# Moving split weights to other SBUF offsets, and streaming tokens in permuted orders in the FFN

## The chip, the cores and the metric

The kernel runs on one NeuronCore of a Trainium2 chip. The metric is the device time of one execution in microseconds (us). Three runs of the kernel before took 1754.56, 1755.35 and 1756.45 us; the median is 1755.35 us. The engines are PE (TensorE; its weight loads are shown apart as PEld), DVE (VectorE), ACT (ScalarE), POOL (GpSimd) and SP (SyncE, which issues nearly all loads).

## The reference, cut to what matters

One layer over 256 tokens of width 2048: two layer norms, modulation from a conditioning vector, grouped-query attention with a window and a context, a convolution branch, gates, a merge, and a SwiGLU feed-forward part of width 5632. All arrays are float32. Nearly all of the arithmetic is in the matrix products, of which the change touches these:

```python
proj = h @ w_in                                   # q, k, v, GLU (a, gt), gates (ga, gc)
y_attn = attn_flat @ lp['w_attn_proj']            # ap
y_conv = conv @ lp['w_conv_proj']                 # cp
mix = (g_attn * y_attn + g_conv * y_conv) @ lp['w_out']      # wo
g, u = jnp.split(h2 @ w_ffn_in, 2, axis=-1)       # fg, fu
ffn = (jax.nn.silu(g) * u) @ w_ffn_out            # fo
```

## The kernel before, in words

Every float32 product is made from three products in float32r (float32 with a shorter mantissa for PE). Each operand is split into `hi`, a copy rounded to float32r (ACT, line 229 for weights, 124 for tokens), and `lo`, the rest (DVE, line 232 or 125). PE then adds hi·hi, hi·lo and lo·hi in PSUM.

The weights come as a stream of units. A unit is 1 MB: four blocks of 128 rows by 512 columns, or two of 128 by 1024. SP loads a unit in two halves into `raw` tiles; ACT and DVE split each half into one tile `hi` and one tile `lo` of 128 partitions by 1024 words. Each of the two kinds has four such slots (`whi`, `wlo`), so two units are split ahead of the one that PE works on. A Python planner writes the order of all engines out: after each unit it places the splits of the unit two ahead and so much convolution work for DVE (`BUDGET`, some 3 us a unit) and rows of the modulation (`ROWS`). The order on each engine is fixed by this; nothing is chosen at run time.

There are two ways to multiply:

- `mm_ws` (lines 248 to 256): the weight block of 128 by 128 is stationary, and the 256 tokens stream through: 48 matmuls of 256 columns for each unit. It serves gt, a, ga, ap, gc, cp and the FFN's fg and fu. The FFN has 22 chunks of 512 columns in the order fg0, fu0, fg1, fu1 and so on to fu10, each of four units.
- `mm_as` (lines 234 to 246): 128 tokens are stationary, and 512 weight columns stream. It serves q and wo, and with two blocks of 512 the last product fo. `kv_piece` (lines 501 to 503) does the same for K and V, once on the tokens (`hhi`, `hlo`) and once on the context (`hc`).

Each matmul has its own weight load, which runs beside the matmul before it. So at any time PE reads two places of SBUF: the operand that streams, and the stationary operand of the next matmul. The start addresses in the built program, modulo 256 bytes, are as follows. All blocks within a tile lie at multiples of 512 bytes, so one number stands for a tile. "Difference" is the stationary operand's start less the streaming one's, modulo 256.

| products | streams | stationary | difference before | difference after |
|---|---|---|---|---|
| gt, a, ga, ap, gc, cp | tokens at 32 | weights at 224, after 96 | 192 | 64 |
| fg, fu: chunks 0 to 15 | tokens at 32 | weights at 224, after 96 | 192 | 64 |
| fg, fu: chunks 16 to 21 | tokens at 32 | weights at 224, after 80, 88, 92, 100, 104, 112 | 192 | 48, 56, 60, 68, 72, 80 |
| q, wo, kv | weights at 224, after 32 | tokens at 32 | 64 | 0 |
| kvc (context) | weights at 224, after 32 | `hc` at 224, after 32 | 0 | 0 |
| fo | weights at 224 | tokens `hr` at 224 | 0 | 0 |
| last products fol, by pieces | weights at 32 or 224 | tokens at 224 or 32 | 192, 0, 64 | 192, 0, 64 |

In the last two pieces of the last product (lines 1015 to 1027, 256 columns each, named `fol`) the weights of units that were kept earlier (`hl`, at 32) stand before those of the ordinary slots (`hi`, `lo`, at 224).

Of the kernel before, what the change touches and what calls it, by code (L numbers as in the profile page):

```python
# [16 lines left out]
P = 128  # L17
# [35 lines left out]
ROWS = (60, 35, 0, 45, 50, 70, 60, 25)
ROW_GAP = 2
G1_PE_ROWS = 8
Z_GAP = 4
# The end: units of the last product held back, and the pieces of the last columns and stores.
LATE = 5
LAST_COLS = ((0, 512), (512, 256), (768, 256))
OUT_COLS = (((0, 1024), (1024, 1024)), ((0, 512), (512, 512), (1024, 512), (1536, 256), (1792, 256)))  # L60
SCHED = {ET.PE, ET.SP, ET.DVE}

# [26 lines left out]
def layer(ctx, tc, x, c, cx, c_ctx, w_mod, b_mod, w_in, attn_sink, conv_w, conv_b, conv_norm_g, conv_norm_b,  # L89
# [36 lines left out]

# [1 line left out]
    cst = cp.tile([P, 1026], F32, name="cst")  # L128
# [40 lines left out]

# [1 line left out]
    units = []  # L171
# [19 lines left out]
    def unit(kind, src, work, post=None, shape=(P, 4, 512)):  # L191
        u = Unit()
        u.kind, u.src, u.work, u.post, u.shape = kind, src, work, post, list(shape)
        u.after, u.fill, u.extra, u.keep, u.direct = [], None, 0.0, False, False
        units.append(u)
        return u
# [15 lines left out]
    def emit_split(u, i, half, defer_lo=False):  # L212
        nk, nc_ = u.shape[1:]
        h = max(1, nk // 2)
        a = h * half
        if half == 0:
            u.hi, u.lo = [], []
            if u.keep:
                u.both = t16([P, 2, nk, nc_], f"hl{i}", F32R)
        if u.keep:  # L220
            hi, lo = u.both[:, 0, a:a + h], u.both[:, 1, a:a + h]
        else:
            hi = sb.tile([P, h, nc_], F32R, name=f"hi{i}_{a}", tag="whi", bufs=2 * SPLITS)
            lo = sb.tile([P, h, nc_], F32R, name=f"lo{i}_{a}", tag="wlo", bufs=2 * SPLITS)
        u.hi += [hi[:, k] for k in range(h)]
        u.lo += [lo[:, k] for k in range(h)]
        src = u.raw[half]
        with tc.high_priority(offset=URGENT):
            act.activation(hi, src, AF.Copy)  # L229
            if defer_lo:  # L230
                return lambda: dve.tensor_sub(lo, src, hi.bitcast(F32))
            dve.tensor_sub(lo, src, hi.bitcast(F32))  # L232
# [15 lines left out]
    def mm_ws(ps, xh, xl, k0, u, first, last):  # L248
        for ct, ki in [(ct, ki) for a in (0, 2) for ct in range(4) for ki in (a, a + 1)]:
            cs = slice(P * ct, P * ct + P)  # L250
            o = ps[ct // 2][:, 256 * (ct % 2):256 * (ct % 2) + 256]
            k, l = k0 + ki, last and ki == 3
            pe.matmul(o, u.hi[ki][:, cs], xh[:, k, :], start=first and ki == 0 and ct % 2 == 0, stop=False,  # L253
                      skip_group_check=True)
            pe.matmul(o, u.hi[ki][:, cs], xl[:, k, :], start=False, stop=False, skip_group_check=True)  # L255
            pe.matmul(o, u.lo[ki][:, cs], xh[:, k, :], start=False, stop=l, skip_group_check=True)  # L256

    def chunk(lst, mul, w, c0, x2, post, name, rate=0, late=False):
# [3 lines left out]
        for q in range(4):  # L262
# [39 lines left out]

# [1 line left out]
    def load_x(src, name):  # L304
# [97 lines left out]

# [1 line left out]
    def mod_head(k0, kind):  # L404
# [39 lines left out]
    def modulate(k0, srcs=(1, 0)):  # L444
        if hT[0] is None:
            hT.v = [t16([P, KT, SEQ], "hhi", F32R), t16([P, KT, SEQ], "hlo", F32R)]
        ks = slice(k0, k0 + 2)
        for s in srcs:
            src = ("x", "ctx")[s]
            if s == 0:  # L450
                hi, lo = hT[0][:, ks, :], hT[1][:, ks, :]
            else:
                if k0 == 0:
                    env["hc"] = t8([P, 2, 2, 2, SEQ], "hc", F32R)
                hi, lo = (env["hc"][:, k0 // 2 % 2, i] for i in range(2))
            xT = env[src + "T"]
            tmp = sg(f"hm{s}{k0}", (P, 2, SEQ))
            for i in range(2):
                k = k0 + i
                dve.tensor_scalar(tmp[:, i, :], xT[:, k, :], scv[:, k, s:s + 1], shv[:, k, s:s + 1],  # L460
                                  op0=OP.mult, op1=OP.add)
            hi_lo(hi, lo, tmp)

# [1 line left out]
    def rope(dst, ps, t):  # L465
# [52 lines left out]
    def kv_unit(k0):  # L518
        order = ((0, 1), (0, 0), (1, 1), (1, 0))

        def work(u):
            for kind, s in order:
                for i in range(2):
                    pieces.append(lambda kind=kind, s=s, i=i: kv_piece(u, k0, i, kind, s))
        return unit("w", wsrc(w_in, k0, OFF_K, 2, 1024), work, shape=(P, 2, 1024))

# [15 lines left out]

# [1 line left out]
    def q_post(j, ps):  # L544
# [67 lines left out]

# [1 line left out]
    rows_start = {}  # L614

    def mod_row(name, c0):
        n = G1_PE_ROWS if name == "g1" else 0

        def place(k):
            """Column block and quarter of the rows of a unit for the tensor engine."""  # L620
            k -= KT - n
            return k // (n // 4), 4 - n // 4 + k % (n // 4)
# [53 lines left out]

# [1 line left out]
    end_of_slot = []  # L678
# [125 lines left out]

# [1 line left out]
    def ap_post(j, ps):  # L806
# [28 lines left out]

# [1 line left out]
    def renorm_x():  # L837
# [119 lines left out]

# [1 line left out]
    def fg_post(j, ps):  # L959
# [102 lines left out]

# [1 line left out]
    rows_make = {n: mod_row(n, D * i) for n, i in (("g1", 2), ("sh2", 3), ("sc2", 4), ("g2", 5))}  # L1064
# [119 lines left out]

# [1 line left out]
    glu[0].after.append(kv_finish)  # L1186
# [27 lines left out]

# [1 line left out]
    state = {"split": 0}  # L1216
# [96 lines left out]
```

## Time and profile before

| what | value |
|---|---|
| time, median of three runs | 1755.35 us |
| profiled execution, span from the first to the last instruction | 1752.4 us |
| median less span | 2.95 us |
| PE busy / DVE busy / ACT busy | 1710.0 / 1261.8 / 770.4 us |
| mean granted TensorE clock | 0.994 of full |
| matmuls of 256 float32r columns by `mm_ws` | 8784 (lines 253, 255, 256 together) |

The profile states the span of its one execution and no second time for it; what lies around the span is taken as the 2.95 us by which the median is longer. The busy time of a matmul in the profile is a modelled length that overlaps its neighbours (281 ns for one of 256 columns). The rate is read from the distance between two starts, or from the number of matmuls in a window.

### The profile page before, as it was taken

What the parts mean: (1) busy time and instruction counts of PE and PEld (TensorE: products, weight loads), DVE (VectorE), ACT (ScalarE), POOL (GpSimd) and SP (SyncE); (2) the same over time, 40 slices, a digit from 0 to 9 for tenths busy, and PEclk for the clock granted to TensorE, in tenths of its full rate; (3) what the DMA queues carried; (4) which work ended last, traced back from release to release, by engine and by line L of the source; (5) the groups of instructions that cost most, each with busy time, mean ns of one, the idle gap of its engine ahead of it and who ended that gap; (6) DMA issues with size and microseconds to landing.
All of it is one profiled execution on the core that took longest, in us unless ns stands there. A gap on an engine that the chain in (4) does not pass through costs nothing.

```text
span 1752.4 us, 29735 instructions
## 1 busy us (share of the span) xinstructions
PE 1710.0 (98%) x12185; PEld 1545.0 (88%) x12185; DVE 1261.8 (72%) x1698; ACT 770.4 (44%) x949; POOL 7.5 (0%) x8
## 2 busy tenths in 40 slices
PE   5999999999999999999999999999999999999997
PEld 3667999777889999999977899999999999888886
DVE  5446699999998899887898648555555544555766
ACT  3222443366664344466334443434343444444451
POOL 0000000000000000000000000000000000000000
PEclk8999999999999999999999999999999999999999
DMA  9996877643347777876899377777777776555561
GB/s 344 326 330 198 275 253 240 193 120 98 108 121 242 249 267 254 285 265 221 316 353 320 102 228 253 230 239 231 237 231 238 232 227 181 192 192 193 193 226 61
DMA packets 190064, 397.10 MB, mean 227 GB/s; under 512 B 11748, under 2 KB 45540, under 8 KB 188644
## 3 DMA queue, kind: packets, MB, share of 16 engines
q1 hardware_dynamic: 188320, 390.20, 68.0%
q10 hardware_dynamic: 1608, 5.01, 0.7%
q8 instruction: 95, 1.56, 0.4%
q14 instruction: 41, 0.34, 0.1%
HBM read 393.06 MB, written 2.10 MB: 225 GB/s over the span
## 4 chain that ended last, share of the span: by engine, by line
PE 91%; DVE 6%; ACT 1%; DMA 1%; issue 1%; SPq 0%; DVEq 0%; ACTq 0%
PE fu L255 5%; PE fu L253 5%; PE fu L256 5%; PE fg L255 5%; PE fg L256 5%; PE fg L253 5%; PE fo L246 4%; PE fo L243 4%; PE fo L244 4%; PE ap L253 2%; PE ga L253 2%; PE gc L256 2%; PE a L253 2%; PE a L255 2%; PE ap L256 2%; PE gc L255 2%
## 5 line engine op out<-in xcount | busy, mean ns | idle before, releaser
L229 ACT ACTIVATE hi<-raw 128x1024 fp32r<-128x1024 f32 x524 | 554.0, 1059 | 729.4 <-PE fu L255 148.3
L232 DVE TENSOR_TENSOR lo<-raw,hi 128x1024 fp32r<-128x1024 f32 x522 | 635.1, 1222 | 313.3 <-ACT hi L229 309.7
L253 PE MATMUL fu<-h2hi,hi 128*128 128x256 f32 x704 | 197.8, 281 | 0.0
L255 PE MATMUL fu<-h2lo,hi 128*128 128x256 f32 x704 | 196.9, 280 | 0.0
L256 PE MATMUL fu<-h2hi,lo 128*128 128x256 f32 x704 | 196.5, 279 | 0.0
L715 DVE SCALAR_TENSOR_TENSOR y<-ub,cwT,y 128x256 f32<-128x256 f32 x480 | 195.5, 477 | 0.0
L256 PE MATMUL fg<-h2hi,lo 128*128 128x256 f32 x688 | 192.9, 280 | 0.4 <-DVE lo L232 0.4
L253 PE MATMUL fg<-h2hi,hi 128*128 128x256 f32 x688 | 193.3, 281 | 0.0
L255 PE MATMUL fg<-h2lo,hi 128*128 128x256 f32 x688 | 193.2, 281 | 0.0
L253 PEld LDWEIGHTS fu<-h2hi,hi 128*128 128x128 f32 x704 | 132.3, 188 | 0.7 <-issue 0.7
L255 PEld LDWEIGHTS fu<-h2lo,hi 128*128 128x128 f32 x704 | 132.1, 188 | 0.7 <-issue 0.7
L256 PEld LDWEIGHTS fu<-h2hi,lo 128*128 128x128 f32 x704 | 131.8, 187 | 0.0
L253 PEld LDWEIGHTS fg<-h2hi,hi 128*128 128x128 f32 x688 | 130.1, 189 | 0.2 <-issue 0.2
L256 PEld LDWEIGHTS fg<-h2hi,lo 128*128 128x128 f32 x688 | 129.5, 188 | 0.6 <-DVE lo L232 0.6
L255 PEld LDWEIGHTS fg<-h2lo,hi 128*128 128x128 f32 x688 | 129.9, 189 | 0.2 <-issue 0.2
L243 PE MATMUL fo<-hi,hr 128*128 128x512 f32 x320 | 124.5, 389 | 0.0
L244 PE MATMUL fo<-lo,hr 128*128 128x512 f32 x320 | 124.5, 389 | 0.0
L246 PE MATMUL fo<-hi,hr 128*128 128x512 f32 x320 | 98.9, 389 | 0.0
L636 DVE SCALAR_TENSOR_TENSOR g<-raw,csil,g 128x1024 f32<-128x1024 f32 x48 | 61.1, 1283 | 28.0 <-DMA raw<-in_w_mod_dram 27.9
L253 PE MATMUL ga<-hhi,hi 128*128 128x256 f32 x256 | 73.1, 286 | 0.0
L253 PE MATMUL a<-hhi,hi 128*128 128x256 f32 x256 | 72.8, 284 | 0.0
L253 PE MATMUL ap<-ahi,hi 128*128 128x256 f32 x256 | 72.8, 284 | 0.0
(287 smaller groups left out, 3794.4 us busy)
## 6 DMA issues: line engine op xcount, KB each, us to landing
raw<-in_w_in_dram SPq DMA_DIRECT2D x176, 512.0 KB, 4.7
raw<-in_w_ffn_in_dram SPq DMA_DIRECT2D x176, 512.0 KB, 4.6
raw<-in_w_mod_dram SPq DMA_DIRECT2D x128, 512.0 KB, 4.3
raw<-in_w_ffn_out_dram SPq DMA_DIRECT2D x88, 512.0 KB, 3.1
wm<-in_w_mod_dram SPq DMA_DIRECT2D x32, 1024.0 KB, 9.2
raw<-in_w_attn_proj_dram SPq DMA_DIRECT2D x32, 512.0 KB, 6.0
raw<-in_w_conv_proj_dram SPq DMA_DIRECT2D x32, 512.0 KB, 4.7
raw<-in_w_out_dram SPq DMA_DIRECT2D x32, 512.0 KB, 5.8
```

What stands on the lines that cost most here:

```text
L229: act.activation(hi, src, AF.Copy)
L232: dve.tensor_sub(lo, src, hi.bitcast(F32))
L243: pe.matmul(o, a, u.hi[ki][:, js], start=f, stop=False, skip_group_check=True)
L244: pe.matmul(o, a, u.lo[ki][:, js], start=False, stop=False, skip_group_check=True)
L246: pe.matmul(o, b, u.hi[ki][:, js], start=False, stop=l, skip_group_check=True)
L253: pe.matmul(o, u.hi[ki][:, cs], xh[:, k, :], start=first and ki == 0 and ct % 2 == 0, stop=False, skip_group_check=True)
L255: pe.matmul(o, u.hi[ki][:, cs], xl[:, k, :], start=False, stop=False, skip_group_check=True)
L256: pe.matmul(o, u.lo[ki][:, cs], xh[:, k, :], start=False, stop=l, skip_group_check=True)
L636: dve.scalar_tensor_tensor(a, u.raw[n].rearrange("p a b -> p (a b)"), csil[:, k, 0:1], a, OP.mult, OP.add)
L715: dve.scalar_tensor_tensor(y[:, k, :], src, w, y[:, k, :], OP.mult, OP.add)
```

## The change

All of it is in where split weights lie, and in the order in which the FFN's matmuls read tokens.

```diff
+SLACK = 64
+WS_SHIFT, AS_SHIFT, HC_SHIFT = 32, 16, 16
+IN_FORM = {2: (2, 4), 3: (2, 8), 4: (2, 16), 5: (2, 32), 6: (2, 64), 7: (4, 4), 8: (8, 4), 9: (16, 4), 10: (2, 2),
+           11: (4, 8), 12: (4, 16), 13: "pairs", 14: "low"}
+IN_SHIFT = {16: 28, 17: 30, 18: 31, 19: 33, 20: 34, 21: 36}
...
-            hi = sb.tile([P, h, nc_], F32R, name=f"hi{i}_{a}", tag="whi", bufs=2 * SPLITS)
-            lo = sb.tile([P, h, nc_], F32R, name=f"lo{i}_{a}", tag="wlo", bufs=2 * SPLITS)
+            hi, lo = (sb.tile([P, h * nc_ + SLACK], F32R, name=f"{n}{i}_{a}", tag="w" + n, bufs=2 * SPLITS)
+                      [:, u.shift:u.shift + h * nc_].rearrange("p (k c) -> p k c", k=h) for n in ("hi", "lo"))
...
     def mm_ws(ps, xh, xl, k0, u, first, last):
-        for ct, ki in [(ct, ki) for a in (0, 2) for ct in range(4) for ki in (a, a + 1)]:
+        order = [(ct, ki) for a in (0, 2) for ct in range(4) for ki in (a, a + 1)]
+        if u.form:
+            step = 2 if u.form == "pairs" else 1
+            low = (1, 2) if u.form != "low" else (2, 1)
+            for z in range(0, 16, step):
+                for n in (0, *low):
+                    for ct, ki in order[z:z + step]:
+                        o = ps[ct // 2][:, 256 * (ct % 2):256 * (ct % 2) + 256]
+                        x = (xh, xl, xh)[n][:, k0 + ki, :]
+                        if isinstance(u.form, tuple):
+                            o, x = (v.rearrange("p (b a c) -> p a b c", a=u.form[0], c=u.form[1]) for v in (o, x))
+                        pe.matmul(o, (u.hi, u.hi, u.lo)[n][ki][:, P * ct:P * ct + P], x, ...
+            return
+        for ct, ki in order:
...
+            u.shift = WS_SHIFT if mul is mm_ws else AS_SHIFT
...
-                    env["hc"] = t8([P, 2, 2, 2, SEQ], "hc", F32R)
+                    hc = t8([P, 2048 + SLACK // 4], "hc", F32R)
+                    env["hc"] = hc[:, HC_SHIFT:HC_SHIFT + 2048].rearrange("p (a b c s) -> p a b c s", a=2, b=2, c=2)
...
-        return unit("w", wsrc(w_in, k0, OFF_K, 2, 1024), work, shape=(P, 2, 1024))
+        unit("w", wsrc(w_in, k0, OFF_K, 2, 1024), work, shape=(P, 2, 1024)).shift = AS_SHIFT
...
+    for n, u in enumerate(ffn):
+        u.shift, u.form = IN_SHIFT.get(n // 4, WS_SHIFT), IN_FORM.get(n // 4)
...
-    nc = _bacc.Bacc("TRN2", target_bir_lowering=False, num_devices=1)
+    nc = _bacc.Bacc("TRN2", target_bir_lowering=False, num_devices=1, dynamic_dma_scratch_size=8192)
```

Shifts count words of 4 bytes. The slots of split weights grow by 64 words, and the room comes from a DMA scratch area at the start of SBUF, which shrinks from 16,384 to 8,192 bytes. With a form (a, c) a matmul still streams the same 256 tokens, but in another order: words 0 to c-1 of every group of a·c words first, then the next c words of every group, and so on; the output in PSUM is written in the same order, so that every word lands where it did. A form (2, 4) reads runs of 4 words and skips 4. Eleven chunks (2 to 12) have such a form.

All other engines have the same instructions in the same order as before; what moves is on PE in the FFN. The first place is the border of chunk 1 (fu0) and chunk 2 (fg1). `fu01` and `fg10` are PSUM tiles, `h2hi` and `h2lo` the parts of the tokens, `hi240` and so on the parts of the weight unit of that number. Before:

```order
L253 MATMUL fu01_10356<-h2hi_9928,hi240_2_10473 128x256
L255 MATMUL fu01_10356<-h2lo_9929,hi240_2_10473 128x256
L256 MATMUL fu01_10356<-h2hi_9928,lo240_2_10474 128x256
L253 MATMUL fg10_10599<-h2hi_9928,hi241_0_10529 128x256
L255 MATMUL fg10_10599<-h2lo_9929,hi241_0_10529 128x256
L256 MATMUL fg10_10599<-h2hi_9928,lo241_0_10530 128x256
```

And now:

```order
L277 MATMUL fu01_10356<-h2hi_9928,hi240_2_10473 128x256
L279 MATMUL fu01_10356<-h2lo_9929,hi240_2_10473 128x256
L280 MATMUL fu01_10356<-h2hi_9928,lo240_2_10474 128x256
L269 MATMUL fg10_10599<-h2hi_9928,hi241_0_10529 128x2x32x4
L269 MATMUL fg10_10599<-h2lo_9929,hi241_0_10529 128x2x32x4
L269 MATMUL fg10_10599<-h2hi_9928,lo241_0_10530 128x2x32x4
```

The sequence is the same; from chunk 2 on the 256 columns are written as 2 passes over 32 groups of 4 words.

The second place is the border of chunk 13 (fu6, form "pairs") and chunk 14 (fg7, form "low"), on PE as well. Before:

```order
L253 MATMUL fu61_13369<-h2hi_9928,hi299_2_13486 128x256
L255 MATMUL fu61_13369<-h2lo_9929,hi299_2_13486 128x256
L256 MATMUL fu61_13369<-h2hi_9928,lo299_2_13487 128x256
L253 MATMUL fg70_13618<-h2hi_9928,hi301_0_13596 128x256
L255 MATMUL fg70_13618<-h2lo_9929,hi301_0_13596 128x256
L256 MATMUL fg70_13618<-h2hi_9928,lo301_0_13597 128x256
```

And now:

```order
L269 MATMUL fu61_13369<-h2hi_9928,hi299_2_13486 128x256 x2
L269 MATMUL fu61_13369<-h2lo_9929,hi299_2_13486 128x256 x2
L269 MATMUL fu61_13369<-h2hi_9928,lo299_2_13487 128x256 x2
L269 MATMUL fg70_13618<-h2hi_9928,hi301_0_13596 128x256
L269 MATMUL fg70_13618<-h2hi_9928,lo301_0_13597 128x256
L269 MATMUL fg70_13618<-h2lo_9929,hi301_0_13596 128x256
```

In chunk 13 two weight blocks go together through each of the three steps; in chunk 14 the product with the weights' `lo` has moved ahead of that with the tokens' `lo`. The number and size of matmuls stay.

## Rows read from the trace of the kernel before

**Rows 1.** The page: busy time of PE; shares of the chain that ended last.

```profile
PE 1710.0 (98%) x12185; PEld 1545.0 (88%) x12185; DVE 1261.8 (72%) x1698; ACT 770.4 (44%) x949; POOL 7.5 (0%) x8
...
PE 91%; DVE 6%; ACT 1%; DMA 1%; issue 1%; SPq 0%; DVEq 0%; ACTq 0%
```

**Rows 2.** Chain by line in 1070 to 1500, 405 to 446 and 860 to 960 us.

```profile
by line: PE fu L255 17.5%; PE fu L253 17.3%; PE fu L256 17.1%; PE fg L255 15.9%; PE fg L253 15.8%; PE fg L256 15.6%; PE g2b L662 0.8%
...
by line: DVE y L715 38.8%; DVE lo L232 20.3%; DVE sm L575 12.1%; PE pv L602 9.0%; PE s L568 4.2%; DVE s L574 3.6%; issue 3.5%; PE pt L596 2.1%; DVE sm L576 1.7%; DVE rope L476 1.6%; DVE scr L469 1.5%; DVE sm L585 1.2%; DVE sm L584 0.6%; DVE
...
by line: PE wo L244 17.3%; PE wo L246 16.4%; PE wo L243 15.9%; DMA raw<-in_w_conv_proj_dram 10.1%; DVE lo L232 9.9%; issue 8.9%; DVE sc L636 5.8%; PE cp L256 3.6%; PE cp L255 3.2%; PE cp L253 3.2%; DVE m L829 2.4%; DVE gc L828 1.8%; DVE mlo
```

**Rows 3.** Groups by line and shape: out<-in, shape, count | busy, mean ns.

```profile
L253 PE MATMUL fu<-h2hi,hi 128*128 128x256 f32 x704 | 197.8, 281 | 0.0
...
L253 PE MATMUL fg<-h2hi,hi 128*128 128x256 f32 x688 | 193.3, 281 | 0.0
...
L253 PE MATMUL gt<-hhi,hi 128*128 128x256 f32 x256 | 72.8, 284 | 0.0
...
L243 PE MATMUL q<-hi,hhi 128*128 128x512 f32 x128 | 53.6, 419 | 0.0
...
L243 PE MATMUL wo<-hi,mhi 128*128 128x512 f32 x112 | 44.4, 397 | 0.0
...
L501 PE MATMUL kv<-hi,hhi 128*128 128x512 f32 x64 | 26.6, 416 | 0.0
```

**Rows 4.** Windows in the FFN: busy (x count) of PE, PEld, DVE, ACT, POOL; PEclk, DMA, GB/s.

```profile
1070.00:1200.00 130.00, 130.00 (x1106) 130.00 (x1105) 75.82 (x66) 50.97 (x50) 0.00 (x0) 1.00 0.77 245
1200.00:1430.00 230.00, 230.00 (x1950) 229.52 (x1950) 127.79 (x110) 92.98 (x94) 0.00 (x0) 1.00 0.74 236
```

**Rows 5.** PE's timeline: start us, us; 132 matmuls between the first two rows.

```profile
286.02 0.28 PE L256 MATMUL a<-hhi,lo 128*128 128x256 f32 x1
...
300.98 0.28 PE L256 MATMUL a<-hhi,lo 128*128 128x256 f32 x1
```

**Rows 6.** PE's timeline in q (20 between) and in fo (6 between).

```profile
358.26 0.40 PE L246 MATMUL q<-hi,hlo 128*128 128x512 f32 x1
...
362.93 0.40 PE L244 MATMUL q<-lo,hhi 128*128 128x512 f32 x1
...
1560.27 0.39 PE L243 MATMUL fo<-hi,hr 128*128 128x512 f32 x1
...
1561.63 0.39 PE L243 MATMUL fo<-hi,hr 128*128 128x512 f32 x1
```

**Rows 7.** PE's timeline, last pieces: 6 matmuls, 3, then 8 between these rows.

```profile
1738.29 0.28 PE L1022 MATMUL fol<-hl,hr 128*128 128x256 f32 x1
...
1739.01 0.29 PE L1022 MATMUL fol<-hi,hr 128*128 128x256 f32 x1
...
1739.37 0.28 PE L1022 MATMUL fol<-hi,hr 128*128 128x256 f32 x1
...
1740.27 0.28 PE L1026 MATMUL fol<-hi,hr 128*128 128x256 f32 x1
```

**Rows 8.** The chain: eight plain float32 matmuls of 512 columns.

```profile
380.81 3.43 PE pv L602 x8
```

**Rows 9.** DVE's split of weights into ordinary slots and into kept tiles.

```profile
L232 DVE TENSOR_TENSOR lo<-raw,hi 128x1024 fp32r<-128x1024 f32 x522 | 635.1, 1222 | 313.3 <-ACT hi L229 309.7 <-PE ap L255 1.6
...
L232 DVE TENSOR_TENSOR hl<-raw,hl 128x1024 fp32r<-128x1024 f32 x10 | 12.0, 1218 | 1.1 <-ACT hl L229 1.1
```

**Rows 10.** Windows of the stretches in which DVE or the DMA queues are nearly full.

```profile
209.00:285.00 76.00, 76.00 (x646) 75.03 (x644) 70.31 (x107) 30.29 (x31) 0.00 (x0) 1.00 0.75 242
...
313.00:446.00 133.00, 132.53 (x582) 97.55 (x581) 127.40 (x260) 76.03 (x129) 0.00 (x0) 1.00 0.45 130
...
524.00:700.00 176.00, 176.00 (x1467) 168.25 (x1465) 160.65 (x244) 72.41 (x75) 0.00 (x0) 1.00 0.76 253
...
860.00:960.00 100.00, 95.08 (x536) 81.06 (x535) 89.14 (x88) 40.91 (x41) 0.00 (x0) 1.00 0.94 337
```

More of the change, by code (lines that the diff above doesn't have):

```diff
@@ L193, in unit @@
         u.kind, u.src, u.work, u.post, u.shape = kind, src, work, post, list(shape)
-        u.after, u.fill, u.extra, u.keep, u.direct = [], None, 0.0, False, False
+        u.after, u.fill, u.extra, u.keep, u.direct, u.shift, u.form = [], None, 0.0, False, False, 0, None
         units.append(u)
@@ L248, in mm_ws @@
     def mm_ws(ps, xh, xl, k0, u, first, last):
-        for ct, ki in [(ct, ki) for a in (0, 2) for ct in range(4) for ki in (a, a + 1)]:
+        order = [(ct, ki) for a in (0, 2) for ct in range(4) for ki in (a, a + 1)]
[9 more added lines that the diff above has]
+                            o, x = (v.rearrange("p (b a c) -> p a b c", a=u.form[0], c=u.form[1]) for v in (o, x))
+                        pe.matmul(o, (u.hi, u.hi, u.lo)[n][ki][:, P * ct:P * ct + P], x,
+                                  start=first and ki == 0 and ct % 2 == 0 and n == 0,
+                                  stop=last and ki == 3 and n == low[-1], skip_group_check=True)
+            return
+        for ct, ki in order:
             cs = slice(P * ct, P * ct + P)
```

## The prediction

> **What bounds the kernel now.** I read the page first: PE is busy 98% of the span, and 91% of the chain that ended last lies on it [rows 1]. Then the chain by stage: in the FFN it is nothing but PE's own matmuls; at 405 to 446 us (the q products with attention) it runs through DVE; at 860 to 960 us half of it is the wo products, and the rest waits for DMA, DVE and issue [rows 2]. So a shorter step from matmul to matmul shortens nearly the whole span, with two exceptions. Third, the step itself. Busy times of a matmul overlap, so I take distances between starts. In the FFN 1106 + 1950 matmuls of 256 columns fill 360 us: 117.8 ns each [rows 4]. At 286 us the same kind of matmul, with the same shapes and addresses modulo 256, runs at (300.98 - 286.02) / 132 = 113.3 ns, for one stretch [rows 5]; by the starts of all matmuls some 280 of the 8784 run at this step. With 512 columns q takes 4.67 / 20 = 233.5 ns and fo 1.36 / 6 = 226.7 ns [rows 6]. The granted clock is 1.00 in all of these windows, so the clock does not make the difference. PE waits for nobody there: it has two speeds for one shape.
>
> Which speed goes with which difference of start addresses (table in the section on the kernel)? 512 columns: 64 goes with 233.5 ns (q), 0 with 226.7 ns (fo). 256 columns: 192 goes with 117.8 ns, and with 113.3 ns in a few stretches. The last pieces of the last product hold the other two cases of 256 columns [rows 7]: with the kept weights against the second tile of tokens (difference 0) six steps take 0.72 us, 120 ns each; then the ordinary slots begin (difference 64), the first three steps take 0.36 us, and from then on eight take 0.90 us, 113 ns each. The step falls to the low value within three matmuls and stays. So where rows can tell, 64 gives the low step for 256 columns and 0 for 512, and those are the differences the change makes.
>
> **The change part by part.** All sums are against the profiled execution, whose span is 1752.4 us; the median of the runs is 2.95 us more, which I add at the end.
>
> 1. Tokens streaming outside the FFN (gt, a, ga, ap, gc, cp; 192 becomes 64). Six products of 3 x 256 matmuls (gt stands for them) are 4608 [rows 3]; less the 280 that are at 113.3 already, about 4330. Each gains 117.8 - 113.3 = 4.5 ns: -19.3 us. [...] I take the low step that rows show.
>
> 2. FFN chunks in natural order (0, 1, 13, 14, 15; 64). 5 x 192, less 48 of the first unit that never went through `mm_ws`, are 912; -4.1 us. That chunks 13 and 14 take the three products in other order moves when `hi` and `lo` slots come free by one matmul, 0.1 us. ACT and DVE are busy 40% and 56% there (92.98 and 127.79 of 230 us [rows 4]), so it costs nothing; without this cover it would be 0.1 us a unit, 1 us in all.
>
> 3. FFN chunks 16 to 21 (48 to 80), 1152 matmuls. No row shows these differences. Bounds: all at 113.3 (-5.2 us), or none better, up to 120 ns as in the case of difference 0 (+2.5 us). I take half of the gain, -2.6 us.
>
> 4. Weights streaming (q, wo, kv; 64 becomes 0). 3 x 128 + 3 x 112 + 3 x 64 = 912 matmuls of 512 columns [rows 3], each 233.5 - 226.7 = 6.8 ns less: -6.2 us. kvc and fo keep difference 0: nothing.
>
> 5. FFN chunks 2 to 12 in permuted order, 11 x 192 = 2112 matmuls. No matmul of before reads or writes a permuted order, so I bound it. [...] Above: the half rate of plain float32, 429 / 2 = 214.5 ns, +96.7 ns each, +204 us. The nearest rows are the same matmuls in natural order (113.3 to 117.8). I split the forms by run length: six forms read runs of 8 words or more (1152 matmuls), where I take 113.3 ns, -5.2 us; five forms read runs of 2 or 4 words (960 matmuls), where I take today's 117.8, 0 us.
>
> [...]
>
> 6. The splits themselves. ACT and DVE write to shifted tiles. Ordinary slots (raw at 32, parts at 224) take 1222 ns on DVE, kept tiles (all at 32) 1218 ns [rows 9], so the position does not matter to them: 0. The smaller scratch area is not used by any load of this kernel that I can see (SP and ACT issue them all): 0.
>
> 7. What takes some back. Where PE speeds up, DVE must follow in its fixed order. It is busy 127.4 of 133 us in q and 70.3 of 76 us before it [rows 10], and the chain already runs on DVE for 41 us [rows 2]. q's 2.6 us would need DVE at 98%; I count most of that as lost, -2 us of gain. At 860 to 960 us the DMA queues are 94% full [rows 10] and the chain waits for a load, so wo's 2.3 us are mostly lost too. Together +4.5 us. The cover here is small: if it were gone altogether, from 209 to 700 us, see the third rival.
>
> Sum: -19.3 - 4.1 - 2.6 - 6.2 - 5.2 + 4.5 = -32.9 us; 1752.4 - 32.9 + 2.95 = 1722.5 us. Own range: 1711 to 1735, from chunks 16 to 21 and the permuted chunks (either fully at the low step, or some 5 ns above today's).
>
> **The rivals.** First, and on the other side: the permuted orders are slow. Place: chunks 2 to 12, where nothing hides PE (its chain is all matmuls [rows 2]). Price: without the 5.2 us of part 5, the rest gains 27.7 us, so from 27.7 / 2112 = 13 ns above 117.8 on average the kernel is slower than before. If only the five forms with runs of 2 or 4 words fell to the half rate, it would be 960 x 96.7 = +93 us: 1815 us; all eleven, about 1932 us. For it: PE reads at full rate only in whole runs in every row I have, and a step that changes with the offsets alone [rows 6, 7] says that reads of SBUF set it. Against: no row shows it. Chance 0.20.
>
> Second: the change does not do what it says. The 113 ns step appears at difference 192 too [rows 5], so it may be a state that a pause before it sets, not the offset. Then all parts are 0 and the time is 1755. Against: both low steps at the differences 64 and 0 hold to the end of their stretch [rows 6, 7]. Chance 0.07.
>
> Third: DVE becomes the bound wherever it is above 90%, that is from 209 to 700 us. The gain there is 4.5 ns x (646 + 1467 and some 350 between) = 11 us, of which about 1 is counted lost already: 1733 us. For it: 160.65 of 176 us and 70.31 of 76 us [rows 10]. Against: each of these leaves 7 to 9% where PE needs 4%. Chance 0.13.
>
> [...] Chance 0.12.
>
> **How the numbers follow.** The forecast has 0.48. A measurement of this kernel cannot tell less than 0.2%, 3.5 us, from no change. Faster: the forecast, the third and the fourth, 0.73. The second counts 0.05 as the same and 0.02 as slower; the first 0.17 slower, 0.03 the same. So 0.73, 0.08, 0.19. The time is the forecast's, 1722.5 us. The range goes from 1706, a little under the fourth rival, to 1770, which takes in the second and a first rival that costs up to about 47 us on the forecast; below lie some 5%, above some 14%.
>
> **What would show it.** In the new profile gt to cp should step at 113.3 ns in all stages, q and kv at 226.7 ns. Chunks 2 to 12 each have one form and 4 units, so windows of one chunk give its price: 21.8 us at 113.3 ns, 22.6 at 117.8, 41 at half rate. Chunks 16 to 21 should tell which offsets are as good as 64. DVE should stay just under PE from 209 to 524 us, and waits of PE for `lo` should not grow beyond a few us. Wrong it would be if the step at 64 stayed at 118, or any form took over 130 ns.

## The result and the profile after

The changed kernel takes 1769.28 us, median of six runs (1765.74 to 1771.41); the kernel before took 1755.05 us (median of six runs, 1750.72 to 1756.68). The ratio is 1.009, 95% interval 1.0066 to 1.0113: slower, where 1722.5 us was predicted. The profiled execution, the fastest of the six, spans 1764.0 us, 11.6 more than before. The time lies inside the range of 1706 to 1770 us, but in the part that stood for the first rival, not for the forecast.

The page after, its busy times and the shares of the chain [rows 1], and DVE's split of weights [rows 9]:

```profile
PE 1717.8 (97%) x12185; PEld 1553.3 (88%) x12185; DVE 1260.7 (71%) x1698; ACT 770.5 (44%) x949; POOL 7.5 (0%) x8
...
PE 87%; DVE 8%; DMA 2%; ACT 1%; issue 1%; SPq 0%; DVEq 0%; ACTq 0%
...
L241 DVE TENSOR_TENSOR lo<-raw,hi 128x1024 fp32r<-128x1024 f32 x522 | 634.1, 1222 | 331.0 <-ACT hi L238 329.1
```

The instructions are the same in number, and the other engines' busy times within 1.1 us. What changed is the step of PE. Below are windows of the changed kernel: gt1 and a1; ga3 and ap3; chunk 9 (fu4) with form (16, 4); chunk 10 (fg5) with form (2, 2); chunks 14 and 15 in natural order at 64; chunk 16 (fg8) at 48. Columns as in rows 4.

```profile
214.00:254.00 40.00, 40.00 (x356) 40.00 (x355) 39.52 (x60) 16.77 (x17) 0.00 (x0) 1.00 0.78 257
644.96:694.96 50.00, 50.00 (x427) 50.00 (x426) 48.66 (x68) 19.50 (x20) 0.00 (x0) 1.00 0.78 256
1191.00:1215.00 24.00, 24.00 (x180) 24.00 (x179) 11.78 (x10) 8.77 (x9) 0.00 (x0) 1.00 0.69 213
1218.00:1258.00 40.00, 40.00 (x175) 36.24 (x174) 11.86 (x10) 7.40 (x7) 0.00 (x0) 1.00 0.40 122
1329.00:1369.00 40.00, 40.00 (x355) 40.00 (x354) 23.37 (x20) 16.35 (x17) 0.00 (x0) 1.00 0.79 249
1373.00:1393.00 20.00, 20.00 (x172) 20.00 (x171) 11.16 (x10) 7.44 (x7) 0.00 (x0) 1.00 0.77 237
```

A window counts every matmul that reaches into it, two to three more than start in it. With that the first row gives 40 / 353 = 113.3 ns a matmul, the second 117.8, the fourth 40 / 173 = 231 ns: half the rate, with PE busy all the time and the granted clock at 1.00. All steps below are distances between starts, averaged over a chunk without its pauses. The border into chunk 10, the first matmul of chunk 11 and two of q (18 steps apart) on PE's timeline of the changed kernel (start, us):

```profile
351.75 0.40 PE L253 MATMUL q<-lo,hhi 128*128 128x512 f32 x1
...
355.84 0.39 PE L253 MATMUL q<-lo,hhi 128*128 128x512 f32 x1
...
1216.28 0.31 PE L269 MATMUL fu<-h2hi,lo 128*128 128x256 f32 x1
1216.42 0.40 PE L269 MATMUL fg<-h2hi,hi 128*128 128x256 f32 x1
1216.63 0.41 PE L269 MATMUL fg<-h2lo,hi 128*128 128x256 f32 x1
1216.86 0.41 PE L269 MATMUL fg<-h2hi,lo 128*128 128x256 f32 x1
...
1260.55 0.32 PE L269 MATMUL fu<-h2hi,hi 128*128 128x256 f32 x1
```

Chunk 10 takes 1260.55 - 1216.42 = 44.13 us where it took 22.61: +21.52. That alone is nearly twice the loss. q steps at 4.09 / 18 = 227.2 ns (233.5 before [rows 6]).

By the starts of the first matmuls of each stage, after less before, in us, beside the prediction's parts:

| part | predicted | measured |
|---|---|---|
| 1: gt, a, ga, ap, gc, cp | -19.3 | -10.0 (ga and ap together +0.4, the others -10.4) |
| 2: natural chunks 0, 1, 13 to 15 | -4.1 | -3.9 |
| 3: chunks 16 to 21 | -2.6 | +1.0 |
| 4: q and wo; kv | -6.2 | -1.7 and -1.2; kv about 0 |
| 5: permuted chunks 2 to 12 | -5.2 | +27.2 (chunk 10 +21.5, the others +5.7) |
| 7: given back | +4.5 | +1.2 (cp3) |
| loads at the start | 0 | -1.0 |
| sum | -32.9 | +11.6 |

Steps of the permuted chunks, by form (a, c), where c is the length of a run in words and a·c the distance from one run to the next: (2, 4) 117.7 ns, (2, 8) 116.7, (2, 16) 121.3, (2, 32) 120.0, (2, 64) 117.8, (4, 4) 114.5, (8, 4) 126.1, (16, 4) 135.2, (2, 2) 229.9, (4, 8) 119.5, (4, 16) 120.0. The six shifted chunks stand at 117.8 to 120.0 ns.

### The profile page after: what moved, and what is told of

The parts are those of the page before. It is cut to its first block, busy times and chain, and to the rows that moved or that the text cites. A ratio compares the mean times of both kernels' runs of the same rounds, so it can differ in the third digit from the quotient of the medians.

```text
span 1764.0 us, 29735 instructions
## 1 busy us (share of the span) xinstructions
PE 1717.8 (97%) x12185; PEld 1553.3 (88%) x12185; DVE 1260.7 (71%) x1698; ACT 770.5 (44%) x949; POOL 7.5 (0%) x8
## 4 chain that ended last, share of the span: by engine, by line
PE 87%; DVE 8%; DMA 2%; ACT 1%; issue 1%; SPq 0%; DVEq 0%; ACTq 0%
PE fg L269 10%; PE fu L269 8%; PE fo L252 4%; PE fo L253 4%; PE fo L255 4%; PE fu L279 2%; PE fu L280 2%; PE fu L277 2%; DVE y L741 2%; PE ga L277 2%; PE ap L277 2%; PE ga L279 2%; PE ap L280 2%; PE ga L280 2%; PE ap L279 2%; DVE lo L241 2%
## 5 line engine op out<-in xcount | busy, mean ns | idle before, releaser
L241 DVE TENSOR_TENSOR lo<-raw,hi 128x1024 fp32r<-128x1024 f32 x522 | 634.1, 1222 | 331.0 <-ACT hi L238 329.1
L269 PE MATMUL fg<-h2hi,lo 128*128 128x256 f32 x448 | 136.0, 304 | 0.1
L269 PE MATMUL fg<-h2hi,hi 128*128 128x256 f32 x448 | 135.7, 303 | 0.0
L269 PE MATMUL fg<-h2lo,hi 128*128 128x256 f32 x448 | 135.7, 303 | 0.0
L269 PE MATMUL fu<-h2lo,hi 128*128 128x256 f32 x384 | 103.5, 283 | 0.0
L269 PE MATMUL fu<-h2hi,hi 128*128 128x256 f32 x384 | 103.4, 283 | 0.0
L277 PE MATMUL fu<-h2hi,hi 128*128 128x256 f32 x320 | 90.6, 283 | 0.0
L279 PE MATMUL fu<-h2lo,hi 128*128 128x256 f32 x320 | 89.4, 279 | 0.0
L269 PEld LDWEIGHTS fg<-h2hi,lo 128*128 128x128 f32 x448 | 86.1, 192 | 1.7 <-DVE lo L241 0.3
L269 PEld LDWEIGHTS fg<-h2hi,hi 128*128 128x128 f32 x448 | 85.8, 192 | 1.4
L269 PEld LDWEIGHTS fg<-h2lo,hi 128*128 128x128 f32 x448 | 85.8, 191 | 1.4
L280 PE MATMUL cp<-yhi,lo 128*128 128x256 f32 x256 | 71.0, 277 | 1.7 <-DVE lo L241 1.7
```

The lines of the kernel that those rows point to most:

```text
L269: pe.matmul(o, (u.hi, u.hi, u.lo)[n][ki][:, P * ct:P * ct + P], x, start=first and ki == 0 and ct % 2 == 0 and n == 0, stop=last and ki == ...
```

## The experiments

Three questions: what the forms cost by themselves, why (2, 2) is slow, and whether the offset is what makes the low step. In what follows "low" is 113.3 ns and "high" 117.8 ns. Six probes were run once each and are read by chunk from their traces: e3 (1855.57 us), e4 (1736.71), e5 (1736.94), e8 (1749.78), e11 (1858.49) and e12 (1928.49).

**e1: no forms, no shifts.**

```diff
-IN_FORM = {2: (2, 4), ...}
-IN_SHIFT = {16: 28, ...}
+IN_FORM = {}
+IN_SHIFT = {}
```

> The changed kernel with all 22 FFN chunks in natural order at difference 64, as chunks 0, 1 and 15 have it; nothing else differs. Theory F (the forms and the other shifts cost it, the offset gains): every FFN chunk takes 113.3 ns a matmul as chunks 0, 1, 13, 14 and 15 did, so 22 chunks gain 0.85 us each against before and the 24.2 us that the FFN lost are replaced by a gain of 18.4; span 1764.0 - 42.6 = 1721.4 us, ratio to before 0.982. Rival S (the step is a state that is set where PE pauses and then kept; offsets only change the odds): somewhere in the FFN the step goes back to 117.8 ns and stays there; span between 1721 and 1739 us, with chunks of both steps at one difference.

Measured: 1725.64 us (five runs, 1723.09 to 1727.86), ratio to before 0.983 (0.981 to 0.985). All 22 chunks stand at the low step. Windows of ga3 and ap3, and of the FFN, in e1:

```profile
655.00:700.00 45.00, 45.00 (x385) 45.00 (x384) 43.88 (x59) 17.31 (x18) 0.00 (x0) 1.00 0.80 264
1100.00:1350.00 250.00, 250.00 (x2209) 250.00 (x2208) 148.07 (x129) 103.41 (x103) 0.00 (x0) 1.00 0.77 243
```

Theory F holds. The forms and shifts together cost 40 us of span (1764.0 to 1723.8), and the offsets alone gain 28.6 us of span against before, nearly the 32.9 that the prediction had for the whole change. ga and ap stay at the high step here too.

**e2: chunk 10 alone put back, e10: chunk 10 alone changed.** e2 drops one entry of the changed kernel's table; e10 is the kernel before with one chunk permuted.

```diff
 e2
-IN_FORM = {..., 10: (2, 2), ...}
+IN_FORM = {... without 10 ...}
 e10
+            return a.rearrange("p (b a c) -> p a b c", a=2, c=2) if u.form else a
...
+    for u in ffn[40:44]:
+        u.form = True
```

> The changed kernel with one chunk put back: chunk 10 (fg5) in natural order at difference 64 instead of runs of 2 words with hops of 4; the other ten permuted chunks and the six shifted ones stay. Theory F: the form of chunk 10 alone costs 229.9 - 113.3 = 116.5 ns x 192 = 22.4 us, so the span is 1764.0 - 22.4 = 1741.6 us and the ratio to before 0.994: the sign of the result turns. Rival C (the slow stretch is where the step that grew over chunks 7 to 9, 114.5, 126.1, 135.2 ns, would have led in any form): chunk 10 stays above 118 ns and the span above 1750 us.

> The kernel before, and chunk 10 (fg5) alone with runs of 2 words and hops of 4, at before's difference of 192; nothing else differs. Theory R (reading tokens in runs of 2 words halves the rate, whatever the offset): chunk 10 at 229 to 233 ns instead of 117.8, 192 x 112 to 115 = 21.5 to 22.1 us; median 1754.65 + 21.8 = 1776.4 us, ratio 1.0123. Rival (it takes the order and the offset of 64 together): less, down to ratio 1.000.

Measured: e2 1742.81 us, ratio 0.993 (0.990 to 0.996); the sign turns with one chunk of 22. e10 1774.02 us, ratio 1.014 (1.009 to 1.019). Windows of e2 in ga3 and ap3 and in chunk 10; then of e10 in chunks 1, 9 and 10, all at difference 192, the last one permuted:

```profile
652.00:692.00 40.00, 40.00 (x356) 40.00 (x355) 39.85 (x56) 16.34 (x17) 0.00 (x0) 1.00 0.79 269
...
1211.00:1232.00 21.00, 21.00 (x188) 21.00 (x187) 12.62 (x11) 8.82 (x9) 0.00 (x0) 1.00 0.76 238
```

```profile
1021.00:1042.00 21.00, 21.00 (x188) 21.00 (x187) 9.62 (x8) 8.95 (x10) 0.00 (x0) 1.00 0.71 197
1202.00:1223.00 21.00, 21.00 (x181) 21.00 (x180) 11.74 (x10) 8.33 (x9) 0.00 (x0) 1.00 0.76 237
1225.00:1267.00 42.00, 42.00 (x184) 37.95 (x184) 12.29 (x10) 8.04 (x9) 0.00 (x0) 1.00 0.43 129
```

In e2 chunk 10 falls to the low step right behind the slow chunk 9, so rival C is out. Four runs of e2 are two pairs, 1737.60 and 1738.80, 1746.82 and 1747.62; the profiled one is the fastest, with ga and ap at the low step (first row), 6.4 us less there than in the changed kernel. So its median, midway between the pairs, meets the expected 1741.6 us of span by chance; but both pairs lie below all nine runs of the kernel before.

In e10 chunk 10 takes 21.53 us more than in the kernel before, as in the changed kernel: the form does it without the offset and without its neighbours. The first row of e10 holds a surprise: chunk 1 runs at the low step at before's difference of 192.

**e3: the reading and the writing side apart.**

```diff
-                            o, x = (v.rearrange("p (b a c) -> p a b c", a=u.form[0], c=u.form[1]) for v in (o, x))
+                            to, tx = ("p (b a c) -> p a b c" if w in u.form[0] else "p (a b c) -> p a b c" for w in "ox")
+                            o = o.rearrange(to, a=u.form[1], c=u.form[2])
+                            x = x.rearrange(tx, a=u.form[1], c=u.form[2])
```

> A probe: each FFN chunk (192 matmuls) has its own order, all at difference 64, with natural chunks between. In some only the tokens are read in the permuted order (the output columns are written in natural order), in some only the output columns are written in it; such outputs have tokens in other places, so the result isn't the reference's. Runs of 2 words with hops of 4: written side alone in chunk 2, read side alone in 3, both in 5; both sides with hops of 8, 32, 128 and 64 words in chunks 6, 7, 16, 20. Theory R (the read side costs: hops through SBUF halve the rate): chunk 3 at 229 ns, chunk 2 at 113 to 118. Theory W (the written side costs): chunk 2 at 229, chunk 3 at 113 to 118. For hops: if the run of 2 words is what costs, chunks 6, 7, 16 and 20 also stand at 229 ns; if it is the hop of 4 words alone, they stand near 113 to 126. The forms (16, 4) in 9 and 10, (8, 4) in 11 and 12, (2, 16) in 14 and 15, (2, 4) in 18 and 19 split in the same way (reading, writing): the side that costs keeps 135, 126, 121, 118 ns, the other falls to 113.

PE's timeline of e3 at the border from chunk 2, (2, 2) in the written side alone, to chunk 3, in the read side alone; then windows of (16, 4) read (chunk 9) and written (chunk 10):

```profile
1046.26 0.28 PE L272 MATMUL fg<-h2lo,hi 128*128 128x256 f32 x1
...
1047.73 0.28 PE L272 MATMUL fg<-h2hi,lo 128*128 128x256 f32 x1
1047.84 0.39 PE L272 MATMUL fu<-h2hi,hi 128*128 128x256 f32 x1
1048.06 0.41 PE L272 MATMUL fu<-h2lo,hi 128*128 128x256 f32 x1
1048.28 0.41 PE L272 MATMUL fu<-h2hi,lo 128*128 128x256 f32 x1
```

```profile
1271.00:1295.00 24.00, 24.00 (x179) 24.00 (x179) 12.01 (x10) 8.39 (x9) 0.00 (x0) 1.00 0.70 217
1297.00:1317.00 20.00, 20.00 (x179) 20.00 (x178) 11.62 (x10) 7.97 (x9) 0.00 (x0) 1.00 0.77 239
```

Writing in runs of 2 words costs nothing (113.4 ns; the last 13 steps before chunk 3 take 1.47 us), reading in them costs everything (229.8 ns). For (16, 4) reading takes 135.1 ns, writing 113.5. (2, 16) read 121.3, written 113.4; (8, 4) read 126.6 and written at the high step; (2, 4) cannot tell, both sides stand at 117.8. With both sides permuted the hops in between hardly matter: 8 words 233.4 ns, 32 words 233.3, 64 words 226.8; only hops of 128 words give 170.0.

**e12: runs that straddle 16 bytes.** If the length of a run counted, moving it would not matter; if aligned blocks of 16 bytes count, a run of 4 words moved by 2 touches two.

```diff
-                        x = (xh, xl, xh)[n][:, k0 + ki, :]
+                        x = (xh, xl, xh)[n].rearrange("p k s -> p (k s)")
+                        at = SEQ * (k0 + ki) + u.form[2] * (-1 if k0 + ki == KT - 1 else 1)
+                        x = x[:, at:at + SEQ]
```

> A probe at difference 64 (plus what the start shifts): permuted reading from tokens that start 2 words (8 bytes) further in some chunks, so that a run of 4 words no longer lies in one aligned block of 16 bytes but in two; the tokens read are two columns off, so the result isn't the reference's. (2, 2) at start 0 and 2 in chunks 2, 3; (4, 4) at 0, 2, 4, 1 words in 4, 5, 6, 17; natural order 2 words further in 7 and 19, unshifted in 16; (2, 4), (16, 4), (8, 4) 2 words further in 8, 10, 18; (2, 8) at 0 and 2 in 11, 12; (4, 16) at 0 and 2 in 13, 14; (2, 64) and (4, 2) 2 words further in 15, 20. Theory B (PE reads blocks of 16 bytes, and what counts is the blocks that a read touches: twice as many for runs of 2): runs of 4 that straddle touch two blocks each, so chunks 5, 8, 10, 17, 18 go to 226 to 234 ns; runs of 8 that straddle touch 3 instead of 2, about 1.5 x 113 = 170 ns in chunk 12; runs of 16 5 instead of 4, about 142 ns in chunk 14; (2, 2) at 2, natural order and (2, 64) stay. Rival N (the number of runs or the hop counts, not where a run lies): the shifted chunks read as the unshifted, 114 to 135 ns for runs of 4, 117 to 120 for 8 and 16.

Windows of e12: (4, 4) at start 0, at 2 words, at 4 words; (2, 8) at 0 and at 2; (4, 16) at 2:

```profile
1118.50:1138.50 20.00, 20.00 (x177) 20.00 (x176) 11.63 (x10) 7.76 (x8) 0.00 (x0) 1.00 0.71 222
1140.00:1182.00 42.00, 42.00 (x187) 38.54 (x186) 12.97 (x11) 8.37 (x9) 0.00 (x0) 1.00 0.43 132
1184.00:1204.00 20.00, 20.00 (x176) 20.00 (x176) 11.56 (x10) 7.66 (x8) 0.00 (x0) 1.00 0.71 221
1343.00:1364.00 21.00, 21.00 (x182) 21.00 (x181) 12.22 (x11) 7.90 (x8) 0.00 (x0) 1.00 0.68 220
1365.00:1396.00 31.00, 31.00 (x186) 31.00 (x185) 12.55 (x11) 8.51 (x9) 0.00 (x0) 1.00 0.53 170
1421.00:1448.00 27.00, 27.00 (x184) 27.00 (x184) 12.34 (x10) 8.01 (x8) 0.00 (x0) 1.00 0.60 191
```

Theory B holds, in size nearly: (4, 4) goes from 114.6 to 226.5 ns with 2 words and back to 115.1 with 4; with 1 word 232.3; (2, 4) 229.9; (16, 4) from 135.7 to 228.1; (8, 4) to 221.0, below the 226 expected; runs of 8 from 116.8 to 168.4 (170 expected); runs of 16 from 120.0 to 148.0 (142). Natural order was to stay and takes 120.0 and 120.3 ns when moved, against 113.4 unmoved in the same run; the moved start also makes the difference 56, which stood at 117.8 in the changed kernel, and 65 blocks for 64 would make that 119.6. (2, 64) was to stay and went from 117.8 to 128.1; 17 blocks for 16 would be 125.2. (2, 2) stays at 230. So the price of a permuted read is mainly the number of 16-byte blocks that its runs touch. Four words, a whole block, are needed for the full rate: runs of two aligned words stand at 229.9 ns (e11), runs of four at 114.6. The distance between the runs has a part in it that the blocks don't explain: runs of 4 take 114.5 ns at 16 words, 126 at 32 and 135 at 64, and runs of 2 fall from 227 ns at 64 words to 170 at 128 (e3). Why stays open.

**e11: the slow forms at other differences.**

```diff
+IN_FORM = {2: (2, 2), 3: (2, 2), 5: (16, 4), 6: (16, 4), 8: (4, 4), ...}
+IN_SHIFT = {2: 0, 3: 16, 5: 0, 6: 16, ...}
```

> A probe with tokens and output columns in permuted orders at other differences than 64, natural chunks at 64 between: (2, 2) at 192, 0 and 32 in chunks 2, 3, 19; (16, 4) at 192 and 0 in 5, 6; (4, 4) at 64, 0, 32, 128, 192 in 8 to 12; (2, 4) at 0 in 14; (8, 8) and (8, 2) at 64 in 15, 16; (4, 2) and (64, 2) at 0 in 18, 20. Theory R (the run length of what is read decides, the difference is second): runs of 2 words at 229 to 233 ns (170 with hops of 128) at every difference, runs of 4 at the values seen at 64 (117.7, 114.5, 135 ns) give or take 5 ns. Rival (the slow orders come from the difference of 64): at 0 and 192 they fall towards 118 to 120 ns.

Windows of e11 in chunks 2 and 3, (2, 2) at the differences 192 and 0:

```profile
1032.00:1074.00 42.00, 42.00 (x185) 37.94 (x184) 20.82 (x14) 8.10 (x9) 0.00 (x0) 1.00 0.53 177
1076.00:1118.00 42.00, 42.00 (x184) 37.96 (x183) 12.89 (x11) 8.02 (x9) 0.00 (x0) 1.00 0.39 117
```

Theory R holds: (2, 2) takes 229.9, 230.0 and 226.7 ns at 192, 0 and 32; (4, 2) 233.2 at 0; (8, 2) 226.5 at 64; (64, 2) 166.7 at 0. (16, 4) takes 133.4 and 134.7 at 192 and 0; (4, 4) stays between 114.4 and 116.7 at all five differences.

**e4: the difference alone; e5: the whole FFN at 192.** Both change only the table of shifts of e1.

> A probe: all FFN chunks in natural order, chunks at difference 64 alternating with chunks at 192, 0, 128, 32, 96, 160, 224, and at the end a row of 192, 0, 128, 32, 96 without 64 between; nothing else differs from the changed kernel. Theory D (the difference of the start addresses decides): each chunk at 64 takes 113.3 ns, 0 takes 120, 192 takes 117.8, the others 113 to 120 each with one value wherever it stands. Rival S (a state that a pause sets and that PE then keeps): no chunk boundary in the FFN has a pause, so 192 and 0 keep the 113.3 ns with which PE comes into them, and all 22 chunks read the same.

> e1 with one thing put back: all 22 FFN chunks at difference 192, as before had them (the larger slots and everything ahead of the FFN stay as in e1). Theory D (64 and 192 both allow two steps, 113.3 and 117.8 ns, and after a pause of PE 64 comes to rest at the low one, 192 nearly always at the high one): the six entries of the FFN end at 117.8, span 1723.8 + 22 x 0.85 = 1742 us. Rival S (which step is taken is chance at the entry, alike for both differences, and e1 was lucky): the chunks stay at 113.3 or fall into two groups, span 1724 to 1736 us.

Windows of e4 in chunks 3 to 6 (differences 64, 0, 64, 128), then 16 and 17 (192, 0):

```profile
1055.00:1075.00 20.00, 20.00 (x179) 20.00 (x178) 13.35 (x12) 8.39 (x9) 0.00 (x0) 1.00 0.86 292
1077.00:1098.00 21.00, 21.00 (x177) 21.00 (x176) 11.58 (x10) 7.76 (x9) 0.00 (x0) 1.00 0.75 235
1100.00:1121.00 21.00, 21.00 (x181) 21.00 (x179) 11.91 (x10) 8.14 (x9) 0.00 (x0) 1.00 0.75 237
1123.00:1143.00 20.00, 20.00 (x171) 20.00 (x170) 10.96 (x10) 7.42 (x7) 0.00 (x0) 1.00 0.75 234
...
1345.00:1365.00 20.00, 20.00 (x179) 20.00 (x178) 11.60 (x11) 8.10 (x8) 0.00 (x0) 1.00 0.76 242
1367.00:1388.00 21.00, 21.00 (x177) 21.00 (x176) 11.30 (x10) 8.33 (x9) 0.00 (x0) 1.00 0.75 232
```

Each expectation holds by half. 0 takes 120.0 ns both times, 32 118.3, 128 118.7 and 119.0; 160 (120.0) and 224 (116.7) stood once; 96 has two values, 120.0 and 118.7. So at 0, 32 and 128 the difference decides as far as two chunks can tell. But 64 and 192 have two steps. Coming out of the 120 ns of difference 0, chunk 5 at 64 stays high to its end; chunk 16, at 192, enters low and stays low; chunk 2, at 192, enters low and turns high at a pause of 1.6 us. In e4 only the weights move, so it can't tell the difference from the weights' own address; for 64 the last product of the kernel before can, where 113 ns came with other addresses (weights at 224, tokens at 32 [rows 7]). In e5 the six entries of the FFN (one after each pause of PE) all came to rest high: 1736.94 us, one run, 11 more than e1's median though its ga and ap ran low (6.4 us less there than in e1; theory D's 1742 us of span had them high). In e1 the same entries, and a seventh, came to rest low. The same two windows as for e1, in e5:

```profile
655.00:700.00 45.00, 45.00 (x399) 45.00 (x398) 44.00 (x60) 19.20 (x19) 0.00 (x0) 1.00 0.81 273
1100.00:1350.00 250.00, 250.00 (x2125) 250.00 (x2124) 142.95 (x123) 99.07 (x99) 0.00 (x0) 1.00 0.74 233
```

The first row answers a question left by e1: up to the FFN the two kernels are the same program, and here ga3 and ap3 run low, with DVE at 44.00 of 45 us. So neither the offset nor DVE held ga and ap at the high step. In the ten profiles with these stages unchanged (the changed kernel, e1 to e5, e7, e8, e11, e12) ga to ap stood high in six and low in four, and a3 before them the other way round each time. As the program is the same up to there in the changed kernel and in e1 to e5, e11 and e12, it doesn't settle which of the two it is.

**e8: many entries.**

```diff
     def mm_ws(ps, xh, xl, k0, u, first, last):
+        if u.pause:
+            pe.transpose(aux(u.pause)[:, 0:P], ident, ident)
```

> e1 with an added float32 transpose of 128 x 128 on PE ahead of each of the FFN's units (nobody reads what it gives), and the FFN's chunks alternately at difference 64 and 192: some 43 entries at each difference, to count which step PE takes after an interruption. Theory D: at 64 most entries settle at 113.3 ns within a few steps, at 192 most at 117.8. Rival S: the same share of 113.3 at both differences.

PE's timeline of e8 at one entry with difference 64:

```profile
1125.88 0.27 PE L258 MATMUL pause<-cst 128*128 128x128 f32 x1
1125.91 0.37 PE L278 MATMUL fg<-h2hi,hi 128*128 128x256 f32 x1
1126.12 0.28 PE L280 MATMUL fg<-h2lo,hi 128*128 128x256 f32 x1
...
1126.59 0.28 PE L281 MATMUL fg<-h2hi,lo 128*128 128x256 f32 x1
...
1131.35 0.28 PE L281 MATMUL fg<-h2hi,lo 128*128 128x256 f32 x1
```

Four steps take 0.47 us (118 ns), then 42 take 4.76 us (113.3 ns). By the last 16 steps of each unit, 15 of 43 entries at 64 end low, 1 of 44 at 192. The direction is theory D's; its "most" at 64 is wrong for this kind of pause. Two things limit the count. All entries at 64 are fg chunks and all at 192 are fu chunks, so it can't tell the difference from the chunk; e1 against e5, with the same chunks, can, for the six entries of e5. And the low entries don't fall at random: in chunks 6, 10, 14 and 18 the same three of the four units end low, and in 4, 8, 12, 16 and 20 none does. So something that returns every fourth chunk has a say; what, no run here shows.

**e6 and e9: steering the entry in ga and ap.** Seven (e6) or fifteen (e9) first halves of units at difference 32.

```diff
+    for n in (2, 4, 6, 8, 11, 13, 21):
+        pairs[n].kick = (8, 0)
```

> e1, and in seven units of the ga and ap products, each the first or next after a pause of PE, the first half (24 matmuls) at difference 32, the second half and all other units at 64. Theory D with memory (the step is kept until something shifts the two streams against each other; in e4 PE came out of every chunk at 32, 128, 96, 160 and 224 at 113.3 ns): after such a half the steps at 64 are 113.3 ns until the next pause, so ga0 to ap3 lose most of the 8 x 0.85 = 6.8 us against a run in which they stand at 117.8, less 7 x 24 x 5 ns = 0.8 us; against e1, which falls into either kind, 0 to 5 us less: median 1720.5 to 1726 us, ratio to before 0.980 to 0.983. Rival C (the other engines' traffic in ga and ap sets the step): 117.8 ns stands in all units of ga and ap at 64, and the median is that of e1 plus 0.8 us, 1726.4 us.

> e6 with more of the halves at difference 32: in ga and ap units 2, 4, 6, 8, 11, 13, 16, 21, 24, 27, 30 of 32, in the FFN units 10, 14, 18 and 83; all else at 64. In e6 six of seven such halves were followed by 113.3 ns, the seventh by 117.8 until gc0. Theory D: most of ga to ap then stands at 113.3; against e1's profile 8 x 0.85 = 6.8 us less 15 x 24 x 5 ns = 1.8 us and what is left of the high step, about 4 us: median about 1721 us, ratio 0.979 to 0.982. Rival (a half at 32 throws PE out of the low step as often as into it): half of the stretches behind the halves at 117.8, in the FFN too, median above 1726 us.

Measured: e6 1722.74 us, ratio 0.982 (0.980 to 0.984); e9 1720.83 us, ratio 0.984 (0.980 to 0.987). The intervals overlap with e1's: none of the three can be told from another. Windows of e9 in ga3 and ap3, and in the FFN:

```profile
655.00:695.00 40.00, 40.00 (x341) 40.00 (x341) 38.84 (x54) 15.97 (x16) 0.00 (x0) 1.00 0.77 260
1105.00:1350.00 245.00, 245.00 (x2164) 245.00 (x2164) 143.67 (x125) 101.33 (x101) 0.00 (x0) 1.00 0.78 245
```

The mechanism I expected fell, though e9's median meets the 1721 us that it gave. Halves at 32 in the middle of the high stretch (ga3 to ap3) left it high each time, and halves in the FFN left it low: the step outlives 24 matmuls at another difference. What the low stretches behind the earlier halves in ga and ap owe to them is open, since e2, e3, e5 and e7 were low there without any.

**e7: the weights' offset put back** in e1.

```diff
-WS_SHIFT, AS_SHIFT, HC_SHIFT = 32, 16, 16
+WS_SHIFT, AS_SHIFT, HC_SHIFT = 32, 0, 0
```

> e1 with the streamed weights put back: q, wo and kv at difference 64 as before had them (the convolution and tokens-streaming products stay). What the weights' offset is worth by itself: the prediction's part 4 less its share of part 7 says 6.2 - 3 = about 3 us; by the stages of e1 it was q 1.7, wo 0.2, the head 0: about 2 us of 6.2, so 1727.5 us and a ratio to before of 0.984. Rival (the products with attention and the wo products are held by VectorE and by loads in either case): no difference to e1 within 1 us, 1725.6 us.

Measured: 1728.27 us, but six runs from 1719.77 to 1743.32: the times settle nothing. By stages q takes 1.7 us longer than in e1 (233.3 against 227 to 228 ns a matmul), kv changes little (233.2 against 231.1). So q's part of the offset is worth 1.7 us, wo's about 1.

## Why the prediction was wrong

The step that failed is part 5, the permuted chunks: "five forms read runs of 2 or 4 words (960 matmuls), where I take today's 117.8, 0 us", and 113.3 ns for the rest. Runs of 2 and 4 were one class, though the half rate for them lay 93 us above the value taken, and no row told between the two. They are different cases: a run of 4 aligned words is a whole block of 16 bytes (114.5 to 135 ns here), a run of 2 is half of one (229.9). The first rival had the mechanism, half rate from reads of SBUF, and the point from which it decides, 13 ns on average over 2112 matmuls; measured, the eleven chunks lie 27.2 / 2112 = 12.9 ns above 117.8. That alone would have left the time about where it was; the kernel got slower because the rest gained 15.6 us and not 27.7. Its 214.5 ns, half of the 3430 / 8 = 429 ns of a plain float32 matmul of 512 columns [rows 8], was near the 229.9 measured. Its price was wrong: it let all five short forms fall together (1815 us) and not one (192 x 112 = 21.5 us). With chunk 10 alone natural the forecast's sign holds (e2). Of the 44.5 us between -32.9 and +11.6, part 5 has 32.4, part 1 9.3 and part 3 3.6. Both signs of being wrong that the prediction named came: (2, 2) and (16, 4) took over 130 ns, and ga and ap stood at 118 ns at 64.

Part 1 had the size of the gain from the offset, 4.5 ns a matmul, right, and its reach wrong: it took the step as set by the difference. At 64 there are two steps, and ga and ap, 1536 matmuls, took the high one: 7 us missing. That is what the second rival said of difference 192 [rows 5], but as a reason for no gain at all; in fact all entries of the FFN came to rest low at 64 (seven in e1) and high at 192 (six in e5). Outside ga and ap 10.4 of some 12.9 us came. The third rival, DVE as the bound from 209 to 700 us, is refuted by the low step with DVE at 39.52 of 40 us in the changed kernel and at 44.00 of 45 us in e5.

The fourth rival, and with it the lower end of the range at 1706 us, needs a step below 113.3 ns. No run shows one: 113.3 ns is the lowest step of a chunk in any order, and the lowest time of any run here is 1717.68 us (e6).

Part 3 failed: no neighbour of 64 showed the low step, not even 60 or 68, in the changed kernel (117.8 to 120.0 ns) or in e2. The bound named there, 120 ns, was what two of the six took. Part 2 held (-3.9 for -4.1), and the other orders of chunks 13 and 14 cost nothing (113.5 and 113.3 ns a matmul in the changed kernel). Parts 4 and 7 give the forecast sum, -2.9 + 1.2 = -1.7 us for -6.2 + 4.5 = -1.7, but by luck. q and wo kept 2.9 us where 0.4 were left to them; DVE took its 1.2 us back in cp3, which part 7 doesn't name; and kv gave nothing. Twelve kv matmuls among the modulation's products take 2.89 us (2.90 before); only the last three stretches of twelve, with nothing but kv and kvc around them, run at 226.7 ns (2.72 us, 2.80 before). Part 6 held: a split takes 1222 ns on DVE in both kernels [rows 9]. For e1 the same working, with all 22 chunks at the low step, gives a span of 1752.4 - 19.3 - 18.8 - 6.2 + 4.5 = 1712.6 us; measured were 1723.8, and 7 of the missing 11 us are ga and ap.

Some smaller slips didn't decide anything. The 2.95 us around the span are too many: in every run of these kernels the time is 1.7 to 1.9 us above its own span. Part 7's 2 us and most of 2.3 make 4.3 at most, not 4.5, and of the chain's 41 us in q some four fifths lie on DVE [rows 2], not all. The ends of the own range, as it is explained, would be about 1716 and 1747 us, not 1711 and 1735.

## What to carry to other kernels

Count the aligned 16-byte blocks that a permuted read of the moving operand touches, not the length of its runs: here a run of 4 aligned words is whole (114.6 ns), and a run of 2 (229.9 ns), or one of 4 off its alignment (226.5 ns), doubled PE's time; runs far apart had other prices (runs of 4 at 64 words 135 ns, runs of 2 at 128 words 170 ns). When bounds of a term lie tens of microseconds apart, split its cases at every size at which the memory could change its mind, instead of giving a class one middle value. When a rate has two values for one shape, find out in one profile whether an address sets it or a history, and price it by how many entries came to rest at which.

## What was not expected of the hardware

- The written side of a matmul, in runs of 2 float32 words, costs nothing (113.4 ns); the read side doubles the step (229.8 ns).
- At differences 64 and 192 of the start addresses modulo 256 the same matmuls have two steps, 113.3 and 117.8 ns, at a granted clock of 1.00. At the entry of e8 shown above the step is taken within some five matmuls after the pause (four steps of 118 ns, then 113.3) and then kept; in e9 it was kept through 24 matmuls at another difference. After a pause 15 of 43 entries at 64 and 1 of 44 at 192 came to rest low in e8. What decides at an entry stays open. ga and ap went both ways (117.8 ns in the changed kernel and in e1, 113.3 in e2 and e5) in programs that are the same up to there, so the instructions alone don't decide it; that the low entries of e8 return every fourth chunk says that it isn't mere chance either.
- Whether the two steps move a whole kernel is open: three of the eleven runs of the kernel before beside e9 took 1739 to 1742 us where the others took 1752 to 1757. That these three had more of the low step is not shown, as no trace of them exists; e10 shows a chunk at 192 in the low step.
